# Opening a two-layer diffusion backbone: where the eight first-half products of the first FFN stand among the slices of the modulation matrix

## The chip, the cores and the metric

The kernel runs on one core of a Trainium2 chip. The metric is the device time of one execution in microseconds (us); lower is better. PE is the matrix engine (PEld its weight loads), ACT the scalar engine, DVE the vector engine, POOL the general engine, SP the engine that issues most of the transfers. Each engine works through its own queue in order.

## The reference

A stream of 512 latent tokens and one of 256 context tokens, each of width 1024, pass two layers; a layer is FFN, token mixer, FFN, each modulated, gated, and closed by a layer norm. Only the very beginning matters here: the modulation of the first FFN, and that FFN's first matrix product.

```python
m = silu(c) @ w_mod[0] + b_mod[0]        # 9 pieces of 1024: shift, scale, gate, ...
h = x * (1.0 + scale) + shift            # scale is piece 1, shift is piece 0
g, u = split(h @ w_in, 2)                # w_in is 1024 x 5632
y = (silu(g) * u) @ w_out
x = layer_norm(ALPHA * x + 0.5 * gate * y)
```

Everything is float32 to near full precision: each factor is split into a rounded part and its rest (`hi` and `lo`), and three products are added, hi by hi, hi by lo, lo by hi.

## The kernel before

**The product of the first FFN.** Of the 768 tokens the first 384 (`HT`, blocks 0 to 2) are one half, the last 384 (blocks 3 to 5) the other. `tile_strassen` (L1093) makes 128 columns of `g` and of `u` at a time for both token halves and both halves of the 1024 inputs with seven products instead of eight. Its operands are sums of blocks of h: `B11`, `B21` (first token half, inputs 0 to 511 and 512 to 1023), `B22` (second token half, second inputs) and `T1` to `T4` (differences of these). One product (`product`, L1030) is 12 matmuls: 4 pieces of 128 inputs, three terms each.

**The opening.** `T1` to `T4` aren't there at first, so the kernel begins with work that needs only `B11` and `B21`: for the first eight tiles f the "first half" `(f, 0)` is `w` by `B11`, the "second half" `(f, 1)` is `w` by `B21`, added to the first in the same PSUM bank. Between them the sum of the first is copied out to SBUF (`v`); after the second, ACT writes `silu` of the whole (`g`). `open_half` (L1047) does one of these. In `start` four of the sixteen are done (`FIRST_OPEN`), in `opening` (L1084) the other twelve (`SECOND_OPEN`). For each of them `slot` (L180) issues what the other engines do meanwhile, in a fixed order: the pending `lo` parts on DVE, an "early" step, the next weight splits (up to a lead of 3), the "post" step of the product, and one step of the generator `combine` (L734). With the first tile's three `T1` blocks made before, `combine` has 13 steps: for each of three token blocks two steps (transposes, four ACT affines; the `T2` block on DVE, its cast on ACT) and then seven that make `T3`, `B22` and `T4`. After the opening tile 0 of the first FFN runs the products T2, T1, T3, B22, T4 with one more step in each slot; what is left of `combine` is done in full right before T4 (L1136).

**Modulation.** To have `B11` and `B21` at all, scale and shift are needed, 2048 columns of `w_mod[0]`, 8 MB. They are read in 32 slices of 128 x 512 (256 KB), a quarter q of both at a time, eight slices a quarter; `gemv` (L1968) multiplies each slice with 4 matmuls, its row of sums is copied by ACT, turned by PE (`vectors`, L1985), and `latent` (L1999) turns the x blocks of two of the eight input pieces, applies scale and shift (ACT one, DVE one) and splits them into `B11` or `B21`. `combine_begin` (L717) does for the second token half what `T1` needs, one token block at a step: four transposes, four ACT affines, a DVE difference, an ACT cast, a DVE rest.

**Weights.** All weight slices, those of `w_mod` too, go through one list in the order of use (`weight_order`, L207): SP loads a slice into one of 6 `raw` buffers, ACT casts it (`hi`), DVE subtracts (`lo`), and a `raw` buffer is free when both have read it; 8 `w` buffers hold the result. In the list of before stand 24 slices of `w_mod`, two first halves, 8 slices of `w_mod`, then the other fourteen halves. The x blocks 0 to 2 come as 12 pieces of 128 KB on POOL's queue at the very start, the blocks 3 to 5 of 512 KB on SP's queue after the second quarter. In `start` the instructions of ACT and DVE are ordered by the framework's scheduler; from `opening` on (`pin(True)`) they stay in program order.

Of the kernel before, what the change touches and what calls it, by code (L numbers as in the profile page):

```python
# [19 lines left out]
NB_CTX = CTX // P  # L20
NB = NB_LAT + NB_CTX
# [20 lines left out]
MRAW_BUFS = 3  # L42
# [22 lines left out]
HALF = 3  # L65
HT = HALF * P
# [27 lines left out]
class Backbone:  # L94
# [112 lines left out]
    def weight_order(self):  # L207
# [3 lines left out]
        io = self.io  # L211
        jobs = []
# [504 lines left out]
    def combine_begin(self):  # L717

        self.halves = []
        self.new_comb("T1")  # L720
        for n in range(HALF):
            b = HALF + n
            bank = self.h_transposes(b, 0)
            h1 = self.z[b][:, 0:512].rearrange("p (k t) -> p k t", t=P)
            self.h_affine(b, 0, bank, False, h1)
            t1 = self.zplace()[:, :].rearrange("p (k t) -> p k t", t=P)
            s = slice(n * P, n * P + P)
            self.dve.tensor_tensor(t1, h1, self.h32[:, 0, :, s], ALU.subtract)
            self.split(self.comb["T1"][:, 0, :, s], self.comb["T1"][:, 1, :, s], t1)
            self.halves.append((h1, t1))  # L730
            yield
        self.made.add("T1")

    def combine(self, keep=False):  # L734
# [3 lines left out]
        cut = lambda t: t[:, :].rearrange("p (k t) -> p k t", t=P)  # L738
        at = lambda n: slice(n * P, n * P + P)
# [12 lines left out]
        for n in range(HALF):  # L752
            b = HALF + n
            banks = [self.h_transposes(b, half) for half in range(int(begun is not None), 2)]
            h2.append(cut(self.z[b][:, 512:1024]))
            if begun:
                h1.append(begun[n][0])
                t1.append(begun[n][1])
            else:
                h1.append(cut(self.z[b][:, 0:512]))  # L760
                self.h_affine(b, 0, banks[0], False, h1[n])
                if keep:
                    self.pool.dma_start(self.kept[n], self.z[b][:, 0:512])
# [11 lines left out]
            t4.append(cut(self.main.tile([P, 512], F32, tag="mraw", bufs=MRAW_BUFS, name="t4")))  # L775
# [268 lines left out]
    def part_bank(self, hold=None, marked=False):  # L1044
        return self.bank(hold, True, marked)[:, 0:HT]

    def open_half(self, f, half):  # L1047
# [12 lines left out]
        return lambda: self.act.activation(g, b1, AF.Silu)  # L1060
# [893 lines left out]
    def start(self):  # L1954


        io, act, dve = self.io, self.act, self.dve
        Q = D // 4
        self.new_h("s")
        A = self.A = self.sm([2, KD], "modA", 2)  # L1960
        B = self.B = self.modT[0][:, :, 0:KD]
        self.new_z(NB)
        for q in range(4):
            for b in range(HALF):
                c = slice(q * Q, q * Q + Q)
                self.nc.gpsimd.dma_start(self.z[b][:, c], io["x"][0, b * P : b * P + P, c])

        def gemv(q):  # L1968
            row = self.bank()
            for n in range(2):  # L1970
                for j in range(4):
                    (w,) = self.weights(1)
                    w = w[:, :, :].rearrange("p x (a b) -> p x a b", b=Q)
                    for a in range(2):
                        k = 2 * j + a
                        o = row[0:4, n * Q : n * Q + Q]
                        self.mm(o, self.csr[:, k], w[:, 0, a], k == 0, False)
                        self.mm(o, self.csr[:, k], w[:, 1, a], False, k == KD - 1)
                    self.release(1)
                    self.pump(2)  # L1980
            rs = self.q(512)
            act.copy(rs[0:4, :], row[0:4, :])
            return rs

        def vectors(q, rs):  # L1985
            ps = self.bank()
            for x in range(4):
                self.tp(ps[:, 4 * x : 4 * x + 4], rs[0:4, x * P : x * P + P])
            ks = slice(2 * q, 2 * q + 2)
            for n, i in enumerate((1, 0)):  # L1990
                js = slice(i * KD + 2 * q, i * KD + 2 * q + 2)
                m = self.modT[0][:, :, js]
                view = ps[:, 8 * n : 8 * n + 8].rearrange("p (k s c) -> p s c k", s=2, c=2)
                dve.tensor_tensor(m, view[:, 0], self.bT[:, js].unsqueeze(1).to_broadcast([P, 2, 2]), ALU.add)
# [4 lines left out]
        def latent(q):  # L1999
            banks = [self.bank(), self.bank()]  # L2000
            for x, ps in enumerate(banks):
                for b in range(HALF):
                    k = 2 * q + x
                    self.tp(ps[:, b * P : b * P + P], self.z[b][:, k * P : k * P + P])

            def finish():
                for x, ps in enumerate(banks):
                    k = 2 * q + x
                    h32 = self.h32[:, k // 4, k % 4]
                    sc, bi = A[:, 0, k : k + 1], B[:, 0, k : k + 1]  # L2010
                    if x == 0:
                        act.activation(h32, ps[:, 0:HT], AF.Identity, bias=bi, scale=sc)
                    else:
                        dve.tensor_scalar(h32, ps[:, 0:HT], sc, bi, ALU.mult, ALU.add)
                    c = self.comb["B11" if k < 4 else "B21"]
                    self.split(c[:, 0, k % 4], c[:, 1, k % 4], h32)

            return finish

        opened = {}  # L2020
        with self.tc.issue_after(self.last_split):
            self.pump()
        def first_open(n):
            post = self.open_half(*FIRST_OPEN[n])
            post()
            self.release(1)
            self.pump(2)

        begin = self.combine_begin()
        for q in range(4):  # L2030
            rs = gemv(q)
            if q > 1:
                first_open(2 * q - 4)
            finish = latent(q)
            vectors(q, rs)
            finish()
            if q == 1:
                for b in range(HALF, NB):
                    src = io["x"][0, b * P : b * P + P] if b < NB_LAT else io["ctx"][0, (b - NB_LAT) * P : (b - NB_LAT) * P + P]
                    self.sp.dma_start(self.z[b], src)  # L2040
            if q == 2:
                next(begin)
                first_open(1)
                next(begin)
                next(begin)
# [284 lines left out]
```

## Time and profile before

| | |
|---|---|
| median of 3 runs | 2795.43 us (2794.66 to 2795.72) |
| the profiled execution, its own time | 2794.23 us |
| its span, first to last instruction | 2790.9 us |
| mean granted clock of PE | 0.998 of full |
| PE / DVE / ACT / POOL busy | 98% / 74% / 46% / 20% of the span |
| transfers | 447.31 MB, mean 160 GB/s |

The span is divided by the profile into 40 slices of some 70 us. PE is busy at 7 tenths in the first of them, 9 or more in all the others. A row of the timeline gives the start, the time to the end of the merged group, engine and line, operation, output and inputs, shape and count, and in brackets the idle time before it and what ended it. Line 89 is the helper through which all pinned instructions pass. A row of the windows gives for each engine its busy time, then PE's granted clock, the busy share of the 16 DMA engines, and what they moved.

### The profile page before, as it was taken

What the parts mean: (1) busy time and instruction counts of PE and PEld (TensorE: products, weight loads), DVE (VectorE), ACT (ScalarE), POOL (GpSimd) and SP (SyncE); (2) the same over time, 40 slices, a digit from 0 to 9 for tenths busy, and PEclk for the clock granted to TensorE, in tenths of its full rate; (3) what the DMA queues carried; (4) which work ended last, traced back from release to release, by engine and by line L of the source; (5) the groups of instructions that cost most, each with busy time, mean ns of one, the idle gap of its engine ahead of it and who ended that gap; (6) DMA issues with size and microseconds to landing.
All of it is one profiled execution on the core that took longest, in us unless ns stands there. A gap on an engine that the chain in (4) does not pass through costs nothing.

```text
span 2790.9 us, 41006 instructions
## 1 busy us (share of the span) xinstructions
PE 2746.1 (98%) x14370; PEld 2481.2 (89%) x14370; DVE 2078.2 (74%) x3601; ACT 1294.0 (46%) x2559; POOL 548.6 (20%) x620
## 2 busy tenths in 40 slices
PE   7999999999999999999999999999999999999998
PEld 5999988888899988899998889999988888888887
DVE  6879989587798876587898659789896698733445
ACT  6544442475655432564444246444432666623321
POOL 1002144212111241100314120013242121000001
PEclk9999999999999999999999999999999999999999
DMA  7444466377766483344456534454594424354352
GB/s 234 142 138 143 138 235 207 111 223 231 220 191 178 131 291 108 119 148 148 137 146 218 174 105 144 144 147 141 170 313 148 148 72 91 130 151 130 112 170 87
DMA packets 408133, 447.31 MB, mean 160 GB/s; under 512 B 29560, under 2 KB 289080, under 8 KB 407928
## 3 DMA queue, kind: packets, MB, share of 16 engines
q1 hardware_dynamic: 371848, 332.77, 38.3%
q0 software_dynamic: 36080, 111.93, 13.2%
q8 instruction: 112, 1.84, 0.3%
q14 instruction: 93, 0.76, 0.1%
HBM read 382.62 MB, written 64.19 MB: 160 GB/s over the span
## 4 chain that ended last, share of the span: by engine, by line
PE 65%; DVE 3%; ACT 2%; issue 2%; POOL 1%; DMA 0%; SPq 0%; DVEq 0%; POOLq 0%; ACTq 0%
PE ps L89 64%; PE pp L89 1%; ACT h L692 0%; POOL rs L203 0%; ACT z L2228 0%; ACT p L1743 0%; DVE nm L1735 0%; DVE z L89 0%; DVE q L1640 0%; DMA mraw<-in_w_mod_dram 0%; POOL acc L474 0%; DVE ss L1609 0%; ACT comb L706 0%; ACT w L172 0%; DVE w L89 0%
## 5 line engine op out<-in xcount | busy, mean ns | idle before, releaser
L89 PE MATMUL ps<-comb,w 128*128 128x384 f32 x6696 | 1172.9, 335 | 5.2 <-DVE w L89 2.5
L89 PEld LDWEIGHTS ps<-comb,w 128*128 128x128 f32 x6696 | 1160.4, 188 | 8.9 <-DVE w L89 3.8
L89 PE MATMUL ps<-w,acts 128*128 128x512 f32 (+1 forms) x3792 | 861.1, 388 | 3.6 <-DVE q L89 3.6
L89 PEld LDWEIGHTS ps<-w,acts 128*128 128x128 f32 x3792 | 707.1, 188 | 149.4 <-DVE q L89 4.5
L89 DVE TENSOR_TENSOR w<-raw,w 128x512 fp32r<-128x512 f32 x643 | 470.7, 740 | 288.0 <-ACT w L89 286.5
L89 ACT CAST w<-raw 128x512 fp32r<-128x512 f32 x643 | 395.1, 621 | 625.2 <-PE ps L89 543.8
L89 DVE SCALAR_TENSOR_TENSOR acc<-mraw,cs,acc 128x512 f32<-128x512 f32 x392 | 280.9, 752 | 23.8 <-DMA mraw<-in_w_mod_dram 23.5
L474 POOL PARTITION_ALL_REDUCE acc<-acc x56 | 205.0, 3666 | 327.2 <-DVE acc L89 300.4
L89 PE MATMUL ps<-h,w 128*128 128x512 f32 (+1 forms) x1152 | 241.4, 372 | 0.2 <-DVE w L173 0.2
L89 PEld LDWEIGHTS ps<-h,w 128*128 128x128 f32 x1152 | 203.2, 188 | 37.7 <-DVE w L173 0.4
L89 POOL DMA_DIRECT2D act<-stage x84 | 48.3, 575 | 903.2 <-DVE stage L89 863.7
L89 POOL DMA_DIRECT2D q<-act x226 | 128.2, 615 | 424.3 <-DVE acts L89 252.6
L89 ACT COPY q<-ps 128x384 f32<-128x384 f32 (+1 forms) x182 | 87.9, 483 | 203.0 <-PE ps L89 203.0
L89 PE MATMUL ps<-w,comb 128*128 128x512 f32 x756 | 173.9, 391 | 1.4 <-ACT ps L89 0.8
L89 DVE TENSOR_TENSOR w<-sums,w 128x512 fp32r<-128x512 f32 x198 | 140.8, 717 | 45.7 <-ACT w L89 45.7
L89 PEld LDWEIGHTS ps<-w,comb 128*128 128x128 f32 x756 | 141.2, 188 | 32.5 <-ACT ps L89 1.8
L89 ACT CAST acts<-q 128x384 fp32r<-128x384 f32 (+1 forms) x262 | 127.6, 519 | 71.1 <-DMA q<-act 54.3
L89 DVE TENSOR_TENSOR acts<-q,acts 128x384 fp32r<-128x384 f32 (+1 forms) x262 | 148.7, 604 | 11.3 <-ACT acts L89 11.0
L89 ACT CAST w<-sums 128x512 fp32r<-128x512 f32 x198 | 122.8, 622 | 40.9 <-DVE sums L353 22.2
L203 POOL TENSOR_TENSOR rs<-ve,mhalf 128x1 f32<-128x1 f32 (+3 forms) x47 | 38.5, 820 | 281.3 <-DVE ve L200 181.2
L173 DVE TENSOR_TENSOR w<-raw,w 128x512 fp32r<-128x512 f32 x101 | 67.3, 688 | 24.5 <-ACT w L172 24.1
L89 DVE TENSOR_TENSOR q<-q,ps 128x384 f32<-128x384 f32 (+1 forms) x69 | 39.6, 574 | 58.0 <-PE ps L89 58.0
(223 smaller groups left out, 2528.8 us busy)
## 6 DMA issues: line engine op xcount, KB each, us to landing
raw<-in_ffn_w_in_dram SPq DMA_DIRECT2D x400, 256.0 KB
mraw<-in_w_mod_dram SPq DMA_DIRECT2D x256, 256.0 KB
raw<-in_ffn_w_out_dram SPq DMA_DIRECT2D x176, 256.0 KB
q<-act POOLq DMA_DIRECT2D x216, 192.0 KB, 4.5
raw<-in_gmlp_w_in_dram SPq DMA_DIRECT2D x132, 256.0 KB
act<-stage POOLq DMA_DIRECT2D x74, 384.0 KB, 3.1
zhat<-z POOLq DMA_DIRECT2D x26, 512.0 KB, 3.0
raw<-in_gmlp_w_out_dram SPq DMA_DIRECT2D x48, 256.0 KB
```

The lines of the kernel that those rows point to most:

```text
L89: return self.tc.keep_in_program_order(f(*args, **kwargs))
L173: self.lows.append((key, lambda: self.dve.tensor_tensor(lo, src, hi.bitcast(F32), ALU.subtract)))
L203: self.last_rstd = self.nc.gpsimd.tensor_tensor(rs, ve, self.mhalf[:, 0:1].to_broadcast([P, n]), ALU.pow).ins
L474: nc.gpsimd.partition_all_reduce(accs[c], accs[c], P, bass_isa.ReduceOp.add)
```

## The change

The two half lists become "all eight first halves" and "all eight second halves". The eight first-half slices stand in the weight list after the 21st, 24th, 27th and 30th slice of `w_mod` and four after the 32nd. `start` is written out as one sequence with ACT and DVE in program order, and with a lead of weight splits for every slice. A first half's bank is given up as soon as its sum is copied to `v`; before the second half, `reopen` copies `v` back from SBUF into a bank, into which the second product is added. x pieces of the third and fourth quarter are loaded on SP's queue between slices instead of on POOL's at the start; blocks 3 to 5 come one at a time after the first three first halves. `combine_begin` is advanced before the first halves 5, 6 and 7 instead of in the third quarter. The differences `t1` are in `mraw` buffers instead of `zraw`, and `t4` takes their place.

```diff
-FIRST_OPEN = [(2, 0), (3, 0), (4, 0), (0, 0)]
-SECOND_OPEN = [
-    *((1, 0), (2, 1), (3, 1), (0, 1), (4, 1), (5, 0)),
-    *((1, 1), (6, 0), (5, 1), (7, 0), (6, 1), (7, 1)),
-]
+FIRST_OPEN = [(f, 0) for f in range(8)]
+SECOND_OPEN = [(f, 1) for f in range(8)]
+FIRST_AT = [21, 24, 27, 30, 32, 32, 32, 32]
...
-        start = quarter(0) + quarter(1) + quarter(2) + first[0:2] + quarter(3) + first[2:]
-        jobs.insert(0, ("u", start))
+        slices = [s for q in range(4) for s in quarter(q)]
+        start, at = [], 0
+        for n, upto in enumerate(FIRST_AT):
+            start += slices[at:upto] + first[n : n + 1]
+            at = upto
+        jobs.insert(0, ("u", start + first[len(FIRST_AT) :]))
...
-            t1 = self.zplace()[:, :].rearrange("p (k t) -> p k t", t=P)
+            t1 = self.main.tile([P, 512], F32, tag="mraw", bufs=MRAW_BUFS, name="t1")
+            t1 = t1[:, :].rearrange("p (k t) -> p k t", t=P)
...
+            if begun:
+                t4.append(t1[n])
+            else:
+                t4.append(cut(self.main.tile([P, 512], F32, tag="mraw", bufs=MRAW_BUFS, name="t4")))
...
+    def reopen(self, f):
+
+        v, g = self.begun[f]
+        b1 = self.part_bank(("b1", f), True)
+        self.act.copy(b1, v)
+        self.begun[f] = v, g, b1
...
+            if not go_on:
+                self.begun[f] = v, g
+                self.unhold(("b1", f))
             return lambda: self.act.copy(v, b1)
...
-            self.slot(post, 2, early=self.seed if n == len(seq) - 2 else None)
+            early = self.seed if n == len(seq) - 2 else None
+            if len(seq) == 8 and n + 2 < len(seq):
+                early = lambda n=n: self.reopen(seq[n + 2][0])
+            self.slot(post, 2, early=early)
...
+        self.pin(True)
...
+        def gemv(*leads):
+            for lead in leads:
+                q, n, j = self.at // 8, self.at % 8 // 4, self.at % 4
...
+                self.release(1)
+                self.flush()
+                self.pump(max(0, lead - len(self.wready)))
+                self.flush()
+                self.at += 1
+
+        def total(q):
+            sums[q] = self.q(512)
+            act.copy(sums[q][0:4, :], rows[q][0:4, :])
+            self.unhold(("row", q))
+            turned[q] = [self.bank(("z", q, x)) for x in range(2)]
+            for x, ps in enumerate(turned[q]):
+                for b in range(HALF):
+                    k = 2 * q + x
+                    self.tp(ps[:, b * P : b * P + P], self.z[b][:, k * P : k * P + P])
...
         def first_open(n):
-            post = self.open_half(*FIRST_OPEN[n])
+            post = self.open_half(*FIRST_OPEN[n], go_on=False)
+            self.flush()
             post()
             self.release(1)
-            self.pump(2)
-
+            self.pump(max(0, 3 - len(self.wready)))
+
+        self.at = 0
+        load_z(0, self.pool)
+        load_z(1, self.pool)
+        self.pump(3)
+        gemv(3, 3, 3, 3, 3, 3, 2, 1)
+        total(0)
+        gemv(2, 2)
+        vectors(0)
+        load_z(2, self.sp)
+        gemv(3, 3, 3, 3, 2, 1)
+        total(1)
+        gemv(1, 1)
+        vectors(1)
+        load_z(3, self.sp)
+        gemv(3, 3, 3)
         begin = self.combine_begin()
...
+        first_open(0)
+        load_block(HALF)
+        gemv(3, 3, 3)
+        total(2)
+        first_open(1)
+        load_block(HALF + 1)
+        gemv(3, 3)
+        vectors(2)
+        gemv(3)
+        first_open(2)
+        load_block(HALF + 2)
+        gemv(3, 3, 3)
+        first_open(3)
+        gemv(3, 3)
+        total(3)
+        first_open(4)
+        vectors(3)
+        next(begin)
+        first_open(5)
+        next(begin)
+        first_open(6)
+        self.reopen(0)
+        next(begin)
+        first_open(7)
+        self.reopen(1)
         next(begin, None)
-        first_open(3)
         self.opening(SECOND_OPEN)
```

`vectors(q)` of after also applies scale and shift to the turned x blocks and splits them (two casts on ACT, then two rests on DVE), which `latent` did before.

More of the change, by code (lines that the diff above doesn't have):

```diff
@@ L774, in combine @@
             yield
-            t4.append(cut(self.main.tile([P, 512], F32, tag="mraw", bufs=MRAW_BUFS, name="t4")))
+            if begun:
+                t4.append(t1[n])
+            else:
+                t4.append(cut(self.main.tile([P, 512], F32, tag="mraw", bufs=MRAW_BUFS, name="t4")))
             sub(t4[n], self.h32[:, 1, :, at(n)], t2)
@@ L1045, in part_bank, with open_half @@
         return self.bank(hold, True, marked)[:, 0:HT]
-    def open_half(self, f, half):
+    def reopen(self, f):
[3 more added lines that the diff above has]
+        self.begun[f] = v, g, b1
+    def open_half(self, f, half, go_on=True):
         if not half:
@@ L1962, in start, with load_z @@
         self.new_z(NB)
-        for q in range(4):
+        def load_z(q, queue):
             for b in range(HALF):
                 c = slice(q * Q, q * Q + Q)
[L1966 to L1979, printed above, removed]
-                    self.pump(2)
-            rs = self.q(512)
-            act.copy(rs[0:4, :], row[0:4, :])
-            return rs
@@ L1985, in vectors, with load_block @@
-        def vectors(q, rs):
+                queue.dma_start(self.z[b][:, c], io["x"][0, b * P : b * P + P, c])
+        def load_block(b):
+            src = io["x"][0, b * P : b * P + P] if b < NB_LAT else io["ctx"][0, (b - NB_LAT) * P : (b - NB_LAT) * P + P]
+            self.sp.dma_start(self.z[b], src)
+        rows, sums, turned = {}, {}, {}
+        def gemv(*leads):
+            for lead in leads:
+                q, n, j = self.at // 8, self.at % 8 // 4, self.at % 4
+                if q not in rows:
+                    rows[q] = self.bank(("row", q))
+                (w,) = self.weights(1)
+                w = w[:, :, :].rearrange("p x (a b) -> p x a b", b=Q)
+                for a in range(2):
+                    k = 2 * j + a
+                    o = rows[q][0:4, n * Q : n * Q + Q]
+                    self.mm(o, self.csr[:, k], w[:, 0, a], k == 0, False)
+                    self.mm(o, self.csr[:, k], w[:, 1, a], False, k == KD - 1)
+                self.release(1)
[3 more added lines that the diff above has]
+                self.at += 1
@@ L1986, in vectors @@
+        def total(q):
[7 more added lines that the diff above has]
+                    self.tp(ps[:, b * P : b * P + P], self.z[b][:, k * P : k * P + P])
+        def vectors(q):
             ps = self.bank()
             for x in range(4):
-                self.tp(ps[:, 4 * x : 4 * x + 4], rs[0:4, x * P : x * P + P])
+                self.tp(ps[:, 4 * x : 4 * x + 4], sums[q][0:4, x * P : x * P + P])
@@ L1997, in vectors @@
                     dve.tensor_scalar(A[:, :, ks], m, 1.0, None, ALU.add)
[L1999 to L2018, printed above, removed]
@@ L2020, in start @@
-        opened = {}
-        with self.tc.issue_after(self.last_split):
-            self.pump()
+            h = []
+            for x, ps in enumerate(turned[q]):
+                k = 2 * q + x
+                h32 = self.h32[:, k // 4, k % 4]
+                sc, bi = A[:, 0, k : k + 1], B[:, 0, k : k + 1]
+                if x == 0:
+                    act.activation(h32, ps[:, 0:HT], AF.Identity, bias=bi, scale=sc)
+                else:
+                    dve.tensor_scalar(h32, ps[:, 0:HT], sc, bi, ALU.mult, ALU.add)
+                self.unhold(("z", q, x))
+                h.append((self.comb["B11" if k < 4 else "B21"], k % 4, h32))
@@ L2023, in first_open @@
+            for c, k, h32 in h:
+                act.copy(c[:, 0, k], h32)
+            for c, k, h32 in h:
+                dve.tensor_tensor(c[:, 1, k], h32, c[:, 0, k].bitcast(F32), ALU.subtract)
         def first_open(n):
-            post = self.open_half(*FIRST_OPEN[n])
+            post = self.open_half(*FIRST_OPEN[n], go_on=False)
+            self.flush()
             post()
             self.release(1)
-            self.pump(2)
-        begin = self.combine_begin()
[L2030 to L2045, printed above, removed]
+            self.pump(max(0, 3 - len(self.wready)))
```

## The prediction

> **What bounds the kernel now.** I read first the page's table of engines and its chain, then the windows, then the timeline of PE's first 130 us.
>
> ```profile
> PE 2746.1 (98%) x14370; PEld 2481.2 (89%) x14370; DVE 2078.2 (74%) x3601; ACT 1294.0 (46%) x2559; POOL 548.6 (20%) x620
> ```
> ```profile
> 0.00:10.00 10.00, 3.43 (x14) 1.33 (x14) 2.65 (x6) 3.68 (x7) 6.96 (x19) 1.00 0.67 207
> 10.00:20.00 10.00, 7.60 (x34) 3.68 (x34) 5.11 (x10) 6.13 (x11) 0.54 (x1) 1.00 1.01 330
> 20.00:30.00 10.00, 8.11 (x63) 4.97 (x62) 9.43 (x21) 7.32 (x15) 0.00 (x0) 1.00 0.85 268
> 30.00:40.00 10.00, 6.50 (x40) 4.31 (x39) 8.19 (x20) 6.83 (x14) 0.00 (x0) 1.00 0.94 306
> 40.00:42.00 2.00, 2.00 (x14) 1.97 (x13) 0.24 (x1) 2.00 (x5) 0.00 (x0) 1.00 1.07 381
> 42.00:44.00 2.00, 2.00 (x21) 1.65 (x20) 1.48 (x3) 2.00 (x7) 0.00 (x0) 1.00 1.12 315
> ```
> ```profile
> 46.07 1.74 PE L89 MATMUL ps<-w,csr 128*4 128x256 f32 x11 [0.57 <-DVE w L173]
> 49.69 0.62 PE L89 MATMUL ps<-comb,w 128*128 128x384 f32 x2 [1.89 <-ACT w L172]
> 50.76 3.26 PE L89 MATMUL ps<-comb,w 128*128 128x384 f32 x10 [0.44 <-DVE w L173]
> ...
> 55.26 4.46 PE L89 MATMUL ps<-comb,w 128*128 128x384 f32 x24
> ...
> 64.17 0.60 PE L89 MATMUL ps<-ident,z 128*128 128x128 f32 x4
> ...
> 69.13 61.09 PE L89 MATMUL ps<-comb,w 128*128 128x384 f32 x351
> ```
> ```profile
> 86.11 0.48 ACT L89 COPY pieces<-ps 128x384 f32<-128x384 f32 x1 [0.87 <-PE ps L89]
> ...
> 88.14 0.48 ACT L89 COPY q<-ps 128x384 f32<-128x384 f32 x1 [1.02 <-PE ps L89]
> ...
> 90.22 0.48 ACT L89 COPY q<-ps 128x384 f32<-128x384 f32 x1 [0.38 <-PE ps L89]
> ```
>
> PE is the bound of the whole. From 69.13 us on it runs 61 us without a gap, so every microsecond by which tile 0 of the first FFN ends earlier or later should reach the end. Before that there are two stages: transfers bound the first (DMA share 0.85 to 1.12 from 10 to 44 us), PE the second. Three marks of before: the last slice of w_mod is multiplied at 46.07 + 1.74 = 47.8 (call this T0). Tile 0's first two product copies follow PE at 86.11 and 88.14, the third at 90.22: 2.05 a product, so tile 0 began at 84.0 and, with five products, ended at 94.3. The question is where those marks come to lie.
>
> **The work on PE does not change much.** Sixteen half products remain sixteen; the four made in the first stage become eight. What the change can win is what PE no longer has to do after T0: before, 14 products (47.8 to 84.0, 36.2 us); after, 12.
>
> **T0.** Bytes ahead of the last w_mod slice. Before: 34 slices of 262 KB and all six x blocks of 524 KB, 8.91 + 3.15 = 12.06 MB. After: 36 slices (four first halves stand before it) and x blocks 0 to 2 in pieces; the lead of 3 splits and 6 raw buffers puts it 9 slices ahead of PE, so on SP's queue blocks 3 and 4 go before it, block 5 behind: 9.44 + 1.57 + 1.05 = 12.06 MB. The same. By the windows before had moved 2.07 + 3.30 + 2.68 + 3.06 + 0.76 = 11.87 MB at 42 us, so the slice landed at 42.6, and PE was 5 us late with it. At the earliest the dip of 20 to 30 us (268 beside 306) goes: 1.2 us earlier, 41.4. At the latest the queues in program order make that dip the rule, 268 from 10 us on: 10 + 9.99/0.268 = 47.3. I take 42.0, near the row as it is.
>
> ```profile
> 5.18 1.32 ACT L172 CAST w<-raw 128x512 fp32r<-128x512 f32 x2 [1.52 <-DMA raw<-in_w_mod_dram]
> ...
> 5.83 1.40 DVE L173 TENSOR_TENSOR w<-raw,w 128x512 fp32r<-128x512 f32 x2 [1.96 <-ACT w L172]
> ...
> 6.58 1.66 PE L89 MATMUL ps<-w,csr 128*4 128x256 f32 x7 [0.35 <-DVE w L173]
> ```
>
> From landing to the multiplication of the rest are 6.58 - 5.18 = 1.4 us. The fourth first half lies two slices (1.6 us) ahead: its product runs from 41.8 to 43.85, then two slices of w_mod, 8 matmuls of 0.15: T0 = 45.0, 2.8 earlier than before. Four first halves run in this stage where two did; the two more (4.1 us on PE, two copies on ACT) hide under the loads, since between 20 and 40 us PE was busy 14.6 of 20 and ACT 14.2. Without that cover they would cost 4.1. The x pieces on SP's queue stand behind slices, eight or more slices ahead of their transposes (6.4 us); I cost them at nothing.
>
> **From T0 to tile 0.** Now ACT is in program order, and `combine_begin`, which ran during the third quarter, lies here.
>
> ```profile
> 35.93 0.82 PE L89 MATMUL ps<-ident,z 128*128 128x128 f32 x6
> 38.04 0.40 PE L89 MATMUL ps<-ident,q 4*128 4x4 f32 x4 [1.29 <-ACT q L1982]
> ```
> ```profile
> 38.48 0.16 DVE L1994 TENSOR_TENSOR modT<-ps,bT 128x4 f32<-128x4 f32 x1 [0.25 <-PE ps L89]
> ...
> 39.14 0.68 DVE L2014 TENSOR_SCALAR h<-ps,modA,modT 128x384 f32<-128x384 f32 x1
> ```
> ```profile
> 60.55 1.51 ACT L89 ACTIVATE z<-ps,modT,modA 128x128 f32<-128x128 f32 x4
> 62.28 0.49 ACT L89 ACTIVATE pieces<-ps 128x384 f32<-128x384 f32 x1 [0.22 <-PE ps L89]
> 62.82 0.62 ACT L89 CAST comb<-q 128x512 fp32r<-128x512 f32 x1
> ...
> 80.03 0.47 ACT L89 COPY acc<-ps 128x384 f32<-128x384 f32 x1
> 80.40 0.62 ACT L89 CAST comb<-z 128x512 fp32r<-128x512 f32 x1
> 80.92 0.48 ACT L89 COPY ps<-pieces 128x384 f32<-128x384 f32 x1
> 81.33 0.62 ACT L89 CAST w<-sums 128x512 fp32r<-128x512 f32 x1
> ```
> ```profile
> 62.09 0.69 DVE L89 TENSOR_TENSOR q<-z,zraw 128x512 f32<-128x512 f32 x1 [0.85 <-ACT z L89]
> 62.82 0.69 DVE L89 TENSOR_TENSOR t<-h,q 128x512 f32<-128x512 f32 x1
> 63.48 0.69 DVE L89 TENSOR_TENSOR comb<-q,comb 128x512 fp32r<-128x512 f32 x1
> ```
>
> Read the start distances in the ACT rows: a copy takes 0.37 of the queue, a cast 0.52, a seed (ps from SBUF) 0.41. Four affines, the DVE difference that waits for them, and the cast that waits for that: 62.82 - 60.55 + 0.52 = 2.8 us, with nothing of the queue behind able to pass.
>
> Counted from T0, PE: transposes 0.82, first half 4 to 2.87, transposes of the sums to 3.3. ACT: the sums' copy, the copy of half 4; DVE's small vectors 0.67, then h and two casts (some 1.55) to 5.5. Then in program order three times (block 2.8, copy 0.37, weight cast 0.52) = 3.7 each, with a seed after the second and the third: the first seed is done at 5.5 + 7.4 + 0.4 = 13.3, the second at 17.4. PE does halves 5, 6, 7 with 4 transposes (0.35) before each and is at 3.3 + 3 x 2.4 = 10.5: it waits 2.8 us for the first seeded bank, runs to 15.3, and waits 2.0 for the second. This is the **new wait of the change**: the seeds are queued behind blocks on ACT, and PE waits for the seeds. From there ACT needs 4.6 us for two slots (two seeds, two casts, two silus taken as copies, affines, T2's cast: 0.82 + 1.04 + 0.74 + 1.45 + 0.52), PE 2 x 2.05 + 0.35 = 4.45: even, no further wait. Tile 0 starts at 17.4 + 7 x 2.05 + 0.7 = 32.4, against 36.2 before: 3.8 less. Without the two waits it would be 27.9.
>
> **Tile 0.** `combine` has 13 steps; before, 12 slots did 12 of them. Eight slots leave five, `T3`, `B22` and `T4`, beside tile 0's products, where DVE also makes the weight differences of tiles 0 and 1.
>
> ```profile
> 92.87 0.55 DVE L89 TENSOR_TENSOR pieces<-pieces,ps 128x384 f32<-128x384 f32 x1
> 93.34 0.55 DVE L89 TENSOR_TENSOR q<-q 128x384 f32<-128x384 f32 x1
> 93.80 0.68 DVE L89 TENSOR_TENSOR w<-sums,w 128x512 fp32r<-128x512 f32 x1
> 94.41 0.69 DVE L89 TENSOR_TENSOR w<-raw,w 128x512 fp32r<-128x512 f32 x1
> ```
>
> A 512-wide DVE operation takes 0.60 of the queue (93.80 to 94.41). The third block's affines end at T0 + 29.3 on ACT (17.4 + two pairs of 4.6 + 2.7); from there 15 such operations stand in DVE's order up to the rest of `T3`: 38.3. The products T2 and T1 end at 36.5, so T3 waits 1.8. Six more operations up to the last rest of `B22`: 41.9, where T3 has ended at 40.35: 1.5. Last, what remains of `combine` is issued behind the "post" of product B22, which waits for that product: add 0.47, add 0.47, three rests of `T4` at 0.60, and the latency of the last: T4 waits about 2.85. Sum 6.2; tile 0 ends at 32.4 + 10.25 + 6.2 = 48.9. Tile 1 finds its weights ready (over the span DVE is busy 74%, which leaves it some 2.6 us in a tile of 10.25), so nothing is added there.
>
> **Sum.** T0 2.8 earlier, tile 0 started 3.8 sooner after it, 6.2 given back: 94.3 becomes 45.0 + 48.9 = 93.9, 0.4 us faster. Nothing later changes: `t1` and `t4` in `mraw` are free again before the fillers' first load after tile 7, and tiles, queues and buffers follow PE as before. The profiled execution of 2794.23 would be 2793.8; the median lies 1.2 above it, so 2795.0.
>
> The granted clock is a term of 0 or 1.7 us.
>
> ```profile
> 50.00:52.00 2.00, 1.56 (x7) 1.25 (x6) 2.00 (x5) 2.00 (x5) 0.00 (x0) 0.78 0.25 75
> 52.00:54.00 2.00, 2.00 (x8) 1.90 (x7) 2.00 (x4) 1.16 (x3) 0.00 (x0) 0.50 0.95 274
> ```
>
> After T0 of before PE stood 1.89 and 0.44 us with two matmuls between, and the clock fell to 0.50 for some 3.4 us: 10 matmuls in 3.26 us instead of 1.7. A wait of 2.8 may do the same, at 1.7 us; the one in the opening would then mostly fall into the wait for the second seed. The Trainium skill ("TensorE: Matmul & The Clock Gate", section "What's actually happening") says that the clock halves after at least one idle window of about 3.4 us; by that rule waits of 2.8 us would cost nothing more. Here the trace differs from the rule, as 2.3 us of standing still within 3 us were enough.
>
> **Rivals.** *The waits are hidden* (faster): if PE reaches the seeded banks later than ACT, or ACT is some 4.5 us sooner because the blocks' chain overlaps, the two waits go (4.5 with the transposes), tile 0 loses only the T4 wait (3.3 less), and T0 comes at 44.4: 2795.0 - 4.5 - 3.3 - 0.6 = 2786.6. For it: before, with 12 slots, the same chain cost PE nothing from 55 us on. Against: the queue order is written out. *The split queue starves the loads* (slower): total, vectors and each copy of a first half hold ACT until PE is done, the casts behind them hold raw buffers, and SP cannot issue; the place is the stretch of 12 to 42 us, the price is the 47.3 above, T0 = 50.3, 5.3 later, and with one fallen clock 7.0: 2802. It decides once the mean rate from 10 us on is under 275 GB/s. For it, the 268 of 20 to 30 us, where DVE and ACT were busiest; against, six buffers cover 4.9 us and one hold is about 2.5. *The change doesn't do what it says*: the bytes ahead of the last slice are the same, first halves run under the loads, but what follows is set by ACT and DVE alone; that is my forecast.
>
> **How the numbers follow.** A measurement of this kernel tells about 0.2%, 5.6 us, from no change. Forecast 0.70, 2795.0 (with its own bounds 2790 to 2800, all within 0.2%); hidden waits 0.19, 2786.6; starved loads 0.11, 2802. So faster 0.19, same 0.70, slower 0.11. The range goes to both rivals: 2787 to 2802.
>
> **What the profile would show.** T0, the last matmuls of w,csr, at 45 (44.4 to 50.3). In ACT's rows seeds (ps from pieces) behind casts of comb from mraw, and PE waiting for an ACT copy 2.8 and 2.0 us before the first two second halves. In tile 0 PE waiting for DVE comb three times, the longest, near 2.9, before T4. From tile 1 on no difference. I am wrong if PE runs from the eighth first half into tile 0 without those gaps, or if the loads' share falls under 0.85 before 40 us.

## The result and the profile after

The changed kernel takes 2821.07 us (median of 5 runs, 2820.61 to 2823.3) against 2795.43 us of the kernel before in the same runs: 25.6 us slower, ratio 1.0092 with a 95% interval of 1.0077 to 1.0106. The prediction was 2795.0 with a range up to 2802. Its profiled span is 2818.4 us. One execution of run x7 below ran at a granted clock of 0.654 and took 3929.37 us; it is left out of every figure of x7.

To see where the time went, I set the matmuls of both traces side by side: both have 14370 records, and from tile 0 on they are the same in the same order. Marks are starts of matmuls, T0 the end of the last one of w_mod; tile 0 ends where tile 1 starts. The delay of the changed kernel against the one before, in us (the profiled executions took 2794.23 and 2821.07, 26.8 apart):

| mark | before, at | after, at | delay |
|---|---|---|---|
| last w_mod matmul (T0) | 47.8 | 53.6 | +5.8 |
| tile 0 starts | 83.8 | 86.9 | +3.1 |
| tile 0 ends | 94.2 | 104.8 | +10.6 |
| before the second FFN of this form (matmul no. 6201) | | | +12.0 |
| in the second FFN of this form (no. 7901) | | | +20.1 |
| in the third (no. 10801) | | | +26.4 |
| the last matmul | 2779.7 | 2806.7 | +27.0 |

So there are two losses: one of about 11 us up to the end of tile 0, where the change is, and one of some 16 us spread over later stages whose code the change doesn't touch.

**The first loss.** The windows of the changed kernel, to lay beside those of before (busy time of PE, PEld, DVE, ACT, POOL, then clock, DMA share, GB/s):

```profile
10.00:20.00 10.00, 7.96 (x48) 3.98 (x46) 6.35 (x14) 5.75 (x10) 0.00 (x0) 1.00 0.91 284
20.00:30.00 10.00, 6.44 (x40) 3.59 (x38) 6.92 (x17) 5.81 (x11) 0.00 (x0) 0.83 0.83 250
30.00:40.00 10.00, 6.71 (x36) 5.15 (x37) 6.15 (x11) 6.70 (x14) 0.00 (x0) 0.83 0.68 213
```

Between 30 and 40 us the loads move 213 GB/s where before moved 306, though ACT and DVE do less. Three timelines show what holds them: ACT's and SP's of the changed kernel, then SP's of the kernel before:

```profile
26.34 0.58 ACT L87 COPY q<-ps 4x512 f32<-4x512 f32 x1 [1.86 <-PE ps L87]
26.83 1.13 ACT L87 CAST w<-raw 128x512 fp32r<-128x512 f32 x2
30.02 0.67 ACT L87 ACTIVATE h<-ps,modT,modA 128x384 f32<-128x384 f32 x1 [2.06 <-DVE modT L87]
...
37.49 0.48 ACT L87 COPY pieces<-ps 128x384 f32<-128x384 f32 x1 [3.24 <-PE ps L87]
37.87 2.18 ACT L87 CAST w<-raw 128x512 fp32r<-128x512 f32 x4
...
42.57 0.48 ACT L87 COPY pieces<-ps 128x384 f32<-128x384 f32 x1 [2.04 <-PE ps L87]
```
```profile
33.53 1.57 SPq L87 DMA_DIRECT2D raw<-in_w_mod_dram  x3
35.33 0.37 SPq L87 DMA_DIRECT2D raw<-in_ffn_w_in_dram  x1
39.24 0.37 SPq L87 DMA_DIRECT2D raw<-in_w_mod_dram  x1
...
45.31 0.37 SPq L87 DMA_DIRECT2D raw<-in_w_mod_dram  x1
```
```profile
34.38 3.39 SPq L89 DMA_DIRECT2D raw<-in_w_mod_dram  x4
```

Read the bracket and then the next row: ACT stands 1.9 to 3.2 us for PE or DVE, and right behind the instruction that waits come casts of weights that are already loaded ("CAST w x4" at 37.87 runs without a gap). While they stand, no raw buffer comes free and SP issues nothing, from 35.7 to 39.2 us for example. It issues the last slice of w_mod at 45.3 us; in before that was done by 37.8. The clock makes the hold longer: PE ran at 0.50 for 3.41 us from 22.5 and again from 32.7 us (the 0.83 in the windows), and the product that the copy at 37.49 waits for took 3.05 us, where the next one took 2.33. And PE's timeline, same kernel:

```profile
22.45 0.37 PE L87 MATMUL ps<-w,csr 128*4 128x256 f32 x1 [2.32 <-ACT w L87]
...
32.22 0.28 PE L87 MATMUL ps<-w,csr 128*4 128x256 f32 x1 [2.60 <-ACT w L87]
...
52.55 1.08 PE L87 MATMUL ps<-w,csr 128*4 128x256 f32 x8
...
63.57 2.01 PE L87 MATMUL ps<-comb,w 128*128 128x384 f32 x10 [0.69 <-DVE w L87]
67.20 2.38 PE L87 MATMUL ps<-comb,w 128*128 128x384 f32 x12 [1.62 <-ACT ps L87]
...
71.30 4.44 PE L87 MATMUL ps<-comb,w 128*128 128x384 f32 x24 [1.28 <-ACT ps L87]
...
92.60 2.38 PE L87 MATMUL ps<-comb,w 128*128 128x384 f32 x12 [1.24 <-DVE comb L87]
96.34 2.21 PE L87 MATMUL ps<-comb,w 128*128 128x384 f32 x11 [1.36 <-DVE comb L87]
100.25 0.44 PE L87 MATMUL ps<-comb,w 128*128 128x384 f32 x1 [1.71 <-ACT comb L87]
101.47 20.55 PE L87 MATMUL ps<-comb,w 128*128 128x384 f32 x107 [0.77 <-DVE comb L87]
```

The two waits for seeds (67.20, 71.30) and the three in tile 0 (92.60, 96.34, then 100.25 with 101.47) are where the forecast had them; T0 is 8.6 us later than forecast. ACT's rows ahead of the first seed (the last row), same kernel:

```profile
62.99 1.51 ACT L87 ACTIVATE z<-ps,modT,modA 128x128 f32<-128x128 f32 x4
65.25 0.62 ACT L87 CAST comb<-t 128x512 fp32r<-128x512 f32 x1 [0.76 <-DVE t L87]
65.78 0.47 ACT L87 COPY zraw<-ps 128x384 f32<-128x384 f32 x1
66.15 0.62 ACT L87 CAST w<-raw 128x512 fp32r<-128x512 f32 x1
66.67 0.48 ACT L87 COPY ps<-pieces 128x384 f32<-128x384 f32 x1
```

**The second loss.** From the groups on the profile's pages of before and after, the casts of weight sums on ACT (198 of them, in all three FFNs of this form). Behind the last bar stands the idle time ahead of them and what ended most of it:

```profile
L89 ACT CAST w<-sums 128x512 fp32r<-128x512 f32 x198 | 122.8, 622 | 40.9 <-DVE sums L353 22.2
```
```profile
L87 ACT CAST w<-sums 128x512 fp32r<-128x512 f32 x198 | 122.7, 621 | 165.5 <-DVE sums L87 164.7
```

The same casts, but ACT stands 165.5 us ahead of them instead of 40.9, and the DVE sum they wait for bears another line: L353, its own, before; L87 after, the helper of the pinned engine. Those sums are issued in `units`, which the diff doesn't touch. That generator takes `dve = self.dve` once, when the first weight is asked for. Before, that was in `start` with DVE unpinned, and it kept the unpinned handle for the whole kernel. After, `pin(True)` stands ahead of it, and the sums of every FFN are in program order. What it costs shows in the timeline of after in the second FFN of this form:

```profile
1409.29 0.62 ACT L87 CAST w<-sums 128x512 fp32r<-128x512 f32 x1 [1.42 <-DVE sums L87]
...
1410.75 0.47 ACT L87 COPY ps<-ps 128x384 f32<-128x384 f32 x1
...
1411.27 0.97 PE L87 MATMUL ps<-comb,w 128*128 128x384 f32 x4 [0.78 <-ACT ps L87]
```

The cast waits for its sum, the seed of T2's bank (ps from ps) stands behind it on ACT, and PE waits for the seed. In before the seed of that product ended 0.7 us ahead of need and PE ran through.

### The profile page after: what moved, and what is told of

Its sections match the earlier page's. It is cut to its first block, busy times and chain, and to the rows that moved or that the text cites. A ratio compares the mean times of both kernels' runs of the same rounds, so it can differ in the third digit from the quotient of the medians.

```text
span 2818.4 us, 41035 instructions
## 1 busy us (share of the span) xinstructions
PE 2754.7 (98%) x14370; PEld 2484.8 (88%) x14370; DVE 2077.2 (74%) x3601; ACT 1301.8 (46%) x2567; POOL 546.3 (19%) x614
## 4 chain that ended last, share of the span: by engine, by line
PE 58%; DVE 7%; ACT 3%; issue 3%; POOL 1%; DMA 1%; SPq 0%; DVEq 0%; ACTq 0%; POOLq 0%
PE ps L87 57%; DVE w L87 1%; ACT w L87 1%; DVE sums L87 1%; DVE acc L87 1%; PE pp L87 1%; DVE raw L87 1%; DVE q L87 1%; DVE comb L87 0%; DVE z L87 0%; POOL rs L201 0%; ACT h L694 0%; ACT z L2281 0%; DVE nm L1754 0%; ACT p L1762 0%
## 5 line engine op out<-in xcount | busy, mean ns | idle before, releaser
L87 PE MATMUL ps<-comb,w 128*128 128x384 f32 x6696 | 1182.5, 336 | 23.1 <-ACT ps L87 12.1
L87 PEld LDWEIGHTS ps<-comb,w 128*128 128x128 f32 x6696 | 1164.0, 189 | 32.1 <-ACT ps L87 15.2
L87 PE MATMUL ps<-w,acts 128*128 128x512 f32 (+1 forms) x3792 | 861.2, 389 | 1.6 <-DVE q L87 1.6
L87 PEld LDWEIGHTS ps<-w,acts 128*128 128x128 f32 x3792 | 707.3, 188 | 147.3 <-DVE q L87 2.5
L87 DVE TENSOR_TENSOR w<-raw,w 128x512 fp32r<-128x512 f32 x687 | 497.0, 735 | 357.3 <-ACT w L87 355.8
L87 ACT CAST w<-raw 128x512 fp32r<-128x512 f32 x687 | 419.8, 620 | 699.0 <-PE ps L87 537.4
L87 DVE SCALAR_TENSOR_TENSOR acc<-mraw,cs,acc 128x512 f32<-128x512 f32 x392 | 282.1, 757 | 22.3 <-DMA mraw<-in_w_mod_dram 22.0
L87 PE MATMUL ps<-h,w 128*128 128x512 f32 (+1 forms) x1152 | 241.4, 372 | 0.2 <-DVE w L171 0.2
L87 PEld LDWEIGHTS ps<-h,w 128*128 128x128 f32 x1152 | 203.3, 188 | 37.6 <-DVE w L171 0.4
L87 POOL DMA_DIRECT2D act<-stage x84 | 48.1, 572 | 916.1 <-DVE stage L87 900.0
L87 POOL DMA_DIRECT2D q<-act x226 | 128.2, 611 | 424.0 <-DVE acts L87 245.7
L87 ACT CAST w<-sums 128x512 fp32r<-128x512 f32 x198 | 122.7, 621 | 165.5 <-DVE sums L87 164.7
L87 PE MATMUL ps<-w,comb 128*128 128x512 f32 x756 | 173.6, 391 | 0.4 <-DVE w L87 0.2
L87 PEld LDWEIGHTS ps<-w,comb 128*128 128x128 f32 x756 | 141.4, 188 | 31.1 <-DVE w L87 1.0
L87 DVE TENSOR_TENSOR w<-sums,w 128x512 fp32r<-128x512 f32 x198 | 140.0, 708 | 36.8 <-ACT w L87 36.8
L87 ACT CAST acts<-q 128x384 fp32r<-128x384 f32 (+1 forms) x262 | 127.8, 519 | 73.6 <-DMA q<-act 60.4
L87 ACT COPY q<-ps 128x384 f32<-128x384 f32 (+2 forms) x187 | 90.2, 482 | 146.0 <-PE ps L87 145.7
L87 DVE TENSOR_TENSOR acts<-q,acts 128x384 fp32r<-128x384 f32 (+1 forms) x262 | 148.7, 604 | 11.8 <-ACT acts L87 11.8
L87 PE MATMUL ps<-w,h 128*128 128x512 f32 x336 | 77.9, 391 | 0.0
L87 DVE TENSOR_TENSOR q<-q,ps 128x384 f32<-128x384 f32 (+1 forms) x69 | 39.4, 571 | 50.6 <-PE ps L87 50.6
```

The source lines that it names most:

```text
L87: return self.tc.keep_in_program_order(f(*args, **kwargs))
```

## The experiments

Each ratio is against runs of the kernel before on the same chip in the same rounds, with its 95% interval. x1 to x4, x5 to x8 and x9 to x11 are three such groups, each on a chip of its own; from one group to another the ratios can be compared, and microseconds only roughly. The marks come from one trace of each kernel. How far they can be trusted shows in kernels that are alike up to T0: 55.6, 56.1 and 52.8 in x1, x4 and x7, but 46.6, 46.7 and 47.3 in x5, x6 and x11.

| run | T0 | tile 0 starts | ends | ratio |
|---|---|---|---|---|
| before | 47.8 | 83.8 | 94.2 | 1 |
| the change | 53.6 | 86.9 | 104.8 | 1.0092 (1.0077 to 1.0106) |
| x1, sums free | 55.6 | 88.7 | 106.1 | 1.0031 (1.0017 to 1.0045) |
| x2, before with sums pinned | 47.9 | 84.1 | 94.8 | 1.0068 (1.0052 to 1.0085) |
| x3, start unpinned | 49.2 | 79.3 | 95.4 | 0.9996 (0.9987 to 1.0005) |
| x4, x1 and combine drained | 56.1 | 89.3 | 103.0 | 1.0021 (1.0012 to 1.0030) |
| x5, x6 and combine drained | 46.6 | 76.7 | 90.2 | 0.9983 (0.9974 to 0.9992) |
| x6, x3 and csr first | 46.7 | 76.8 | 93.7 | 1.0002 (0.9993 to 1.0011) |
| x7, x1 and seeds early | 52.8 | 86.1 | 103.6 | 1.0032 (1.0019 to 1.0045) |
| x8, x6, halves behind | 41.6 | 79.4 | 95.0 | 1.0006 (0.9997 to 1.0015) |
| x9, x1, ACT alone pinned | 54.3 | 87.3 | 103.4 | 1.0031 (1.0020 to 1.0042) |
| x10, x1, DVE alone pinned | 55.0 | 89.5 | 105.5 | 1.0032 (1.0022 to 1.0042) |
| x11, x5 and two more steps | 47.3 | 77.5 | 90.5 | 0.9979 (0.9970 to 0.9988) |

### The sums of the weights: x1 and x2

```diff
# x1, on the changed kernel, in units
-        dve, w = self.dve, None
+        dve, w = self.nc.vector, None
# x2, on the kernel before, in units
-        dve, w = self.dve, None
+        dve, w = Pinned(self.tc, self.nc.vector), None
```

> The changed kernel with one difference: the weight sums of the generator units (four DVE operations for each tile of a product with sums) are issued through the unpinned DVE, as in the kernel before, instead of in program order. Theory A (the early pin(True) was taken over by the generator for the whole kernel, so that its sums stand in program order in all three FFNs of this form): the steps of the delay after tile 0, 0.2 to 2.2 us each and 15.5 us in sum, go; 2821 - 15.5 = 2805.5, between 2803 and 2809. Rival B (other banks or buffers since the opening, or the clock): the steps stay, 2818 to 2822.

> The kernel before with one difference: the same weight sums in program order from the first one on. Theory A: the delay appears here without any other part of the change, at the same places in the second and third FFN (0.9, 1.4, 2.2 us at every seventh tile, 1.5 in each opening): 2795.4 + 12 to 17, 2807 to 2813. Rival B: 2795 to 2797.

x1 took 2806.01 us, 8.4 over before's 2797.59 of these runs: of the 25.6 us, 17 are gone. x2, the kernel before with nothing but that line changed, took 2814.47, 16.9 over by the medians, 19 by its ratio, and a little more than the 2807 to 2813 expected. The two agree within their intervals, from either side. x2 also shows the steps of delay at the same matmuls and of the same size as the change: 0.94, 1.39 and 2.14 us at numbers 7296, 7548 and 7800 in the second FFN (the change: 0.94, 1.39, 2.17), and the same rows:

```profile
1403.58 0.62 ACT L89 CAST w<-sums 128x512 fp32r<-128x512 f32 x1 [1.42 <-DVE sums L89]
...
1405.04 0.47 ACT L89 COPY ps<-ps 128x384 f32<-128x384 f32 x1
...
1405.56 0.62 PE L89 MATMUL ps<-comb,w 128*128 128x384 f32 x2 [0.78 <-ACT ps L89]
```

Between tile 0 and the second FFN x2 loses 5.0 us in its trace, where the change lost 1.4; why isn't shown. In x1 none of the three steps is left, and the group of casts on its page is back at before's idle time:

```profile
L87 ACT CAST w<-sums 128x512 fp32r<-128x512 f32 x198 | 122.9, 622 | 41.0 <-DVE sums L355 22.3
```

Other banks or buffers after the opening, the rival, would have left x1 at 2818 and x2 at 2795.

### The order of the queues in `start`: x3, x6, x9, x10

```diff
# x3, on the changed kernel (the sums are free too, as the generator begins unpinned)
-        self.pin(True)
         io, act, dve = self.io, self.act, self.dve
# x6, on x3
-        self.pump(3)
+        with self.tc.issue_after(self.last_split):
+            self.pump(3)
# x9, on x1 with the same issue_after
         self.pin(True)
+        self.dve = self.nc.vector
# x10, the same
         self.pin(True)
+        self.act = self.nc.scalar
```

> The changed kernel without pin(True) at the beginning of start: ACT and DVE are ordered by the scheduler up to the opening, and the weight sums are free for the whole kernel too. Theory C (program order makes ACT wait for PE with weight casts behind it, so raw buffers stay full and loads stop): the last slice of w_mod is multiplied at 45 to 49 us instead of 53.6, and the time is 2805.5 - 4 to 8 = 2797 to 2802. Rival D (the place of the slices in the list and the bytes set that time): 52 to 54 us, 2804 to 2807, like the run with free sums alone.

> The changed kernel with an unpinned start, and the first three weight splits held behind the split of csr, as the kernel before held its first splits. Theory C2 (in the unpinned start the first matmuls of w_mod waited until 14.7 us for csr, behind weight splits on ACT and DVE, which left raw buffers full and the loads at 252 GB/s from 10 to 20 us; without that the bytes set T0): first matmul at 5 to 7 us, T0 45 to 47 us instead of 49.2, the time 2 to 4 us below the unpinned start alone, 0.998 to 0.999 of the kernel before. Rival D2 (order and bytes of the list set T0 whatever the queues do): T0 48.5 to 50, no change.

> The run with free sums, in start only ACT in program order, DVE ordered by the scheduler (the first splits behind csr's). If it is ACT's order that holds the loads (its copies of sums and halves and its h wait for PE and DVE, with weight casts behind them), T0 stays at 52 to 56 us and the time at 1.002 to 1.004 of the kernel before. If it is DVE's order, T0 falls to 46 to 49 and the time to 0.999 to 1.001.

> The other half: in start only DVE in program order, ACT ordered by the scheduler. If ACT's order holds the loads, T0 at 46 to 49 us and 0.999 to 1.001 of the kernel before, as x6_unpinned_csr; if DVE's order does, T0 at 52 to 56 and 1.002 to 1.004; if each does part, T0 near 50 in both.

With ACT and DVE ordered by the scheduler T0 comes at 49.2 (x3) instead of 55.6 (x1), just past the 45 to 49 expected, and the time falls from 1.0031 to 0.9996 (2796.14 us, where 2797 to 2802 were expected): the place of the slices, which is the same in both, isn't what made T0 late. In x3 something else held it: its first matmul of w_mod came only at 14.67 us, when the split of csr had at last been issued behind weight splits. With csr first (x6) the first matmul is at 5.79, the loads run at 303, 294 and 305 GB/s from 10 to 40 us, and T0 is 46.7. There ACT's cast of the last slice of w_mod waits for the load itself:

```profile
44.11 0.62 ACT L170 CAST w<-raw 128x512 fp32r<-128x512 f32 x1 [0.69 <-DMA raw<-in_w_mod_dram]
```

So with the queues free that slice lands at 44.1 us. In the changed kernel, where SP issues it only at 45.3, its cast starts at 50.25. In time x6 and x3 can't be told apart (the intervals overlap), though in the profiles tile 0 starts 2.5 us and ends 1.7 us earlier in x6; there the expected 2 to 4 us failed to show.

x9 and x10 were meant to name the engine. Each blames its own engine: in order on ACT alone or on DVE alone, T0 is 54.3 or 55.0 and the time 1.0031 or 1.0032, as with both. So it isn't one engine's order; either is enough, and together they cost no more. PE's timeline of x9, then of x10:

```profile
21.76 0.28 PE L87 MATMUL ps<-w,csr 128*4 128x256 f32 x1 [2.12 <-ACT w L87]
...
31.40 0.28 PE L87 MATMUL ps<-w,csr 128*4 128x256 f32 x1 [2.40 <-ACT w L87]
```
```profile
23.00 3.11 PE L87 MATMUL ps<-w,csr 128*4 128x256 f32 x15 [3.50 <-DVE w L87]
...
34.80 1.66 PE L87 MATMUL ps<-w,csr 128*4 128x256 f32 x7 [5.58 <-DVE w L87]
```

A slice is ready and its buffer free only when both have been at it, so one queue in which splits stand behind waiting instructions is enough. With DVE in order it is DVE's `lo` part, behind the rests of comb that wait for ACT and the small vectors that wait for PE. From the waits of x10 up to 55 us (in total, times, longest):

```profile
DVE comb L87 <- ACT comb L2049: 6.0, 3, 3.0
DVE modT L87 <- PE ps L87: 2.9, 2, 1.6
```

### The halves among the slices: x8

```diff
# x8, on x6, with start's calls moved to match
-FIRST_AT = [21, 24, 27, 30, 32, 32, 32, 32]
+FIRST_AT = [32, 32, 32, 32, 32, 32, 32, 32]
```

> As x6_unpinned_csr, with all eight first halves behind the last slice of w_mod, none among the slices. If the loads bound the stage and PE has room in it, as the prediction took it, T0 comes some 3 to 4 us earlier (1.05 MB less ahead of it) and four products (8.3 us) more follow it: tile 0 starts 3 to 5 us later than in x6_unpinned_csr, and so the end. If the halves among the slices hold the stage up as long as they save, no difference (within 1 us).

T0 comes 5.1 us earlier (41.6), tile 0 starts 2.6 later and ends 1.3 later than in x6, and the time is 2799.65 against 2797.33, with overlapping intervals. T0 moved by more than the 3 to 4 us expected and tile 0's start by less than the 3 to 5. The bytes account for T0: in x8 one x block of 0.52 MB is issued behind the last slice (at 35.0 us, the slice at 34.0) that x6 issues ahead of it (37.3 and 38.0), so that with the four halves 1.57 MB less lie ahead, some 5.2 us at the 305 GB/s of x6's window from 30 to 40 us. So PE does have room under the loads for four products, as the prediction took it: they cost their bytes. But the gain at tile 0's start is only 2.6 us, and half of it is lost again in tile 0.

### The seeds and the rest of combine: x7, x4, x5, x11

```diff
# x7, on x1
         first_open(5)
+        self.reopen(0)
+        self.reopen(1)
         next(begin)
         first_open(6)
-        self.reopen(0)
         next(begin)
         first_open(7)
-        self.reopen(1)
# x4, on x1; x5, on x6
+        for _ in self.combining or ():
+            pass
+        self.combining = None
         step(b2, "B22", True, None, second)
-        for _ in self.combining or ():
-            pass
-        self.combining = None
# x11, on x5, in opening
             self.slot(post, 2, early=early)
+            if len(seq) == 8 and n > 5:
+                next(self.combining)
```

> The run with free sums (start pinned), and the first two seeds issued right behind first half 5, ahead of two of the three blocks of combine_begin, instead of behind them. If the place of the seeds in ACT's order makes the waits of 0.7, 1.6 and 1.3 us before and between the first second halves, they go and the time is 3 to 3.6 us below the run with free sums. If it is ACT's whole work in this stage, in whatever order, PE waits a product or two later for the next seed or cast: within 1.5 us of that run.

> As the run with free sums, and in tile 0 what is left of combine is issued ahead of product B22 instead of behind its post step. If the wait before T4 is made by the rests of T4 standing behind the add that waits for B22, it falls from 2.5 us (1.71 and 0.77, with the half clock that follows) to under 0.5, and the time is 2 to 4.5 us below the run with free sums. If DVE's load alone makes it, the wait moves ahead of B22 and nothing is won (within 1 us).

> As the run x6_unpinned_csr, and with what is left of combine issued ahead of product B22. If the two effects add, 3 to 4 us below x6_unpinned_csr: 0.9965 to 0.998 of the kernel before of the same runs, faster than both kernels. If the wait before T4 is hidden once tile 0 comes earlier, within 1 us of x6_unpinned_csr.

> As x5_unpinned_csr_drained, with one step of combine more in each of the last two slots of the opening, so that T3 and B22 are begun two slots sooner. If the waits of 0.8 and 1.3 us before T3 and B22 in tile 0 come from the place of these steps, they go, and the time is 1 to 2 us under x5_unpinned_csr_drained (0.9975 to 0.998 of before). If DVE's work up to there makes them, they stay or move ahead to T2: within 0.7 us of it.

x7 (2805.55 us, 1.0032) stays with x1 (2806.01, 1.0031): the wait for the seed is gone, and PE waits for a weight in its place. PE's timeline of x7:

```profile
62.72 2.37 PE L87 MATMUL ps<-comb,w 128*128 128x384 f32 x12 [0.70 <-DVE w L87]
67.23 2.01 PE L87 MATMUL ps<-comb,w 128*128 128x384 f32 x10 [2.14 <-DVE w L87]
...
70.92 4.09 PE L87 MATMUL ps<-comb,w 128*128 128x384 f32 x22 [0.89 <-DVE w L87]
```

0.70 + 2.14 + 0.89 = 3.7 us, where x1 waits 0.69 for a weight and 1.62 and 1.29 for seeds, 3.6. ACT's whole queue in this stage makes the wait, as the second alternative had it; the seeds only happened to stand where PE met it. In x6, where the scheduler fills the time in which ACT waits for DVE's difference, 0.52 and 0.41 are left.

Issuing the rest of combine ahead of product B22 takes 3.4 us off x1 (x4, 2802.56; the intervals overlap) and 4.8 off x6 (x5, 2792.50, intervals apart; expected were 3 to 4). PE's timeline of x6, then of x5:

```profile
82.12 2.38 PE L87 MATMUL ps<-comb,w 128*128 128x384 f32 x12 [0.78 <-DVE comb L87]
85.73 2.20 PE L87 MATMUL ps<-comb,w 128*128 128x384 f32 x11 [1.24 <-DVE comb L87]
89.64 0.44 PE L87 MATMUL ps<-comb,w 128*128 128x384 f32 x1 [1.71 <-ACT comb L87]
90.85 21.43 PE L87 MATMUL ps<-comb,w 128*128 128x384 f32 x113 [0.76 <-DVE comb L87]
```
```profile
81.98 2.36 PE L87 MATMUL ps<-comb,w 128*128 128x384 f32 x12 [0.78 <-DVE comb L87]
85.60 26.62 PE L87 MATMUL ps<-comb,w 128*128 128x384 f32 x148 [1.26 <-DVE comb L87]
```

The wait of 1.71 and 0.76 before T4 is gone (in x4 0.19 is left), those before T3 and B22 are what they were. Behind that wait x6's clock falls to half for one stretch, from 91.9 us, and x5's doesn't, so that some of the 4.8 us is the clock's. Two more steps in the opening (x11) don't remove the two that are left: 2791.88 (0.9979), not to be told from x5. PE then waits in four places, 0.53, 0.42, 0.79 and 0.53, for ACT and DVE, 2.3 us in all where x5 waits 2.0. That speaks for the work of the two engines and against the place of one step.

x5 and x11 beat both kernels: 0.9983 and 0.9979 of before, some 5 us, with intervals that end below 1.

## Why the prediction was wrong

**What failed, first: "Nothing later changes".** The prediction looked for what the change does to buffers, fillers and queues after tile 0, and put that term at nothing ("tiles, queues and buffers follow PE as before"). It took the early `pin(True)` for an order of the opening stages alone. But the handle is copied by a generator that lives as long as the kernel. This is 17 of the 25.6 us (x1, x2), and no rival of the prediction covered it.

**Second: T0.** The term was 45.0; measured are 53.6. The bytes ahead of the last slice weren't the error: SP issues blocks 3 and 4 before it and block 5 behind it, as forecast, and with queues free (x6) the loads have moved 11.09 MB by 40 us, before 11.11. There the slice lands at 44.1 instead of 42.0 and T0 is 46.7. The step that failed is "I take 42.0, near the row as it is", which gave the loads of the pinned kernel the rate of an unpinned one. The rival "the split queue starves the loads" named the mechanism, but as ACT's alone, with a chance of 0.11 and T0 of 50.3. Its rate, 268 GB/s, was too kind: 284, 250 and 213 in the three windows from 10 to 40 us, 249 on average, under the 275 at which it was to decide. The prediction's own sign of being wrong, a DMA share under 0.85 before 40 us, showed: 0.83 and 0.68.

**Right: from T0 to tile 0.** 33.2 us measured, 32.4 forecast, with the seeds behind blocks on ACT and two waits for them. The two seeded products begin 13.6 and 17.7 us after T0, where the forecast had the seeds done at 13.3 and 17.4. PE got there later than forecast, so that the waits of 2.8 and 2.0 came as 0.69 (for a weight) and 1.62, then 1.28. x7 confirms the cause, ACT's queue, and corrects the reading: it isn't the place of the seeds.

**Right: tile 0 gives back.** Forecast 6.2 us in three waits of 1.8, 1.5 and 2.85; measured 7.5 more than before's tile, in waits of 1.24, 1.36 and 2.48, together 5.1. The half clock behind them, 3.41 us at 0.50, is 1.7 of the rest, the term that the prediction had left at 0 or 1.7. x4 and x5 show that the last of the waits is the order of the rest of combine behind B22's post; x11 speaks for the others being the engines' work.

**Half right: the cover.** PE has room under the loads (x8), but what the spread brings, 2.6 us at tile 0's start, is smaller than what tile 0 then costs: 16.9 us in x6, 10.4 in before. That eight slots instead of twelve are the reason is argued from the rows (PE waits for T3, B22 and T4); no run had the spread with twelve slots.

The sum of the prediction, no change within 0.2%, is what x6 shows (1.0002): the change without the pin. Tile 0 even ends at 93.7 there, as against 93.9 in the forecast. In part that is luck: T0 is 1.7 us later, the way to tile 0 2.3 us shorter (30.1, with waits of 0.52 and 0.41) and tile 0 0.4 longer, in a kernel whose queues aren't those that the prediction described. Of the change as made, 17 us are the sums; the rest, 8.4 us, goes when `start` is unpinned as well.

## What to carry to other kernels

Where a helper pins or unpins an engine, look for who keeps a copy of its handle: a generator or a closure made under the new state carries it into stages that the diff never names, and the line in the profile's rows (a helper's instead of its own) shows it at once. In a stage that the loads bound, keep instructions that wait for another engine from standing ahead of the casts and subtractions that free load buffers, on each of the engines that must touch a buffer. And work that is spread over slots has to be counted in slots: twelve slots become eight, and what no longer fits is paid by the next tile, where the order behind a waiting post step decides.

## What the runs showed of the hardware

The granted clock falls after shorter standstills than the idle window of about 3.4 us that the Trainium skill gives ("TensorE: Matmul & The Clock Gate", section "What's actually happening"); the prediction had seen that in before, and the change shows it again. Two windows of the changed kernel, the first over the wait before T4, the second from near its end on:

```profile
97.60:101.00 3.40, 1.38 (x7) 0.81 (x5) 2.42 (x5) 1.24 (x3) 0.00 (x0) 1.00 0.00 0
101.00:104.40 3.40, 2.94 (x9) 2.94 (x10) 2.21 (x4) 1.22 (x2) 0.00 (x0) 0.50 0.14 41
```

PE was busy for 1.38 of 3.4 us, no single gap was longer than 1.71 us, and the next 3.4 us ran at 0.50. In x6 it falls too, at 91.9 us. In x3, with waits of the same size in tile 0 (0.84, 1.24, 1.71 and 0.77), it doesn't, and its tile 0 takes 16.1 us against 16.9 in x6: in these traces such waits cost nothing more in one run and about 1 us more in another. What decides it isn't shown.
